# The attention's two query buffers in a pool of their own, over the index scores instead of over the layer input

## The chip, the cores and the metric

The kernel runs on one core of a Trainium2 chip. The metric is the device time of one execution in microseconds (us); the time of a kernel is the median of several runs on the same chip. The engines are named as in the profile: PE is TensorE, DVE is VectorE, ACT is ScalarE, POOL is GpSimd, SP is SyncE (here it only issues DMA transfers). Every engine takes its own instructions in the order in which the program holds them.

## The reference, cut to what matters

The model is a trunk of two layers over 1024 tokens of width 1024. Layer 0 projects the input once and feeds two mixers side by side: A, a delta-rule recurrence (RWKV-7, 8 heads of 64), and B, a sparse attention (8 query heads of 64 over one shared key and value, the 256 best keys of each query chosen by index scores). Layer 1 is a gated linear attention. The change concerns part B:

```python
def dsa_mix(q, ckv, qi, ki, wi, pos, kvn_g, wuk, wuv):
    c = rms_norm(ckv, kvn_g)
    k, v = partial_rope(c @ wuk, pos), c @ wuv
    q = partial_rope(q.reshape(Bn, T, B_HEADS, B_HEAD_DIM), pos)
    for each block of 128 queries:
        score = einsum('bqh,bqhs->bqs', wib, relu(einsum('bqhd,bsd->bqhs', qib, ki)))
        score = where(adm, score, -inf)                 # keys of this chunk of 64 and of those before
        vals, idx = top_k(score, 256)                   # the 256 best keys of each query
        s = einsum('bqhd,bqkd->bqhk', qb, k[idx]) * 64 ** -0.5
        out = einsum('bqhk,bqkd->bqhd', softmax(s), v[idx])
```

## The kernel before, in words

All is written in one function, `trunk`, with tiles from pools; a scheduler orders the instructions of each engine at build time by a model of its own, except where the code pins PE's order (`inorder`). Memory on the chip is handed out as on two stacks, one from each side. A pool that opens when another has closed takes over its place, and the first writer of a new tile waits until the last reader of the old tiles under it is done.

Layer 0 goes through these stages:

1. The input is transposed and split into a high and a low part, `xh` and `xl` (32 KB of each partition each, pool `big`). The index scores of query blocks 2 to 7 go into one tile `sc` (16.5 KB, pool `scp`). The queries of the attention are written to DRAM, `d_q`.
2. On PE, columns of the input projection follow one another: a block of weights is loaded (`wcols`, tile `craw`), split, and multiplied with `xh` and `xl` (`mm_cols`, lines 183 to 185, into the PSUM tile `dn`). Meanwhile DVE and ACT search the threshold of the 256 best scores in `sc` and write the masks `bias_s` (lines 670 to 747).
3. The last group of projections (`j = 3`, lines 750 to 765) gives the last head pair of part A. `operands` and `bonus` write its pieces to DRAM with DMAs that SP issues (`d_ar`, `d_bk`, `d_bd`, `d_bv`, `d_vt`; lines 534 to 613). Two gates come last (`gate`, lines 497 to 503: PE into `dn`, a tanh on ACT at line 501, a product on DVE at line 502 into the one buffer `sg`, then a DMA to `d_gate`).
4. The pools of these stages close, and the stage of the attention and the recurrence opens. On the right side lie `dsa` (keys, values, masks), then `scp`, then `big`, then the projection's weights. `dsa` stays. The attention's pool `at` opens in the place of the other three. It holds a small mask, the two query buffers `qT` (4 KB each), the score rows `p0` and `p1` and more. The recurrence's pool `rw` opens on the left side, over the tiles of stage 3; its first tiles (`GM`, `zi`, `XI`, `gn`, the first `RUV`) lie where `sg` lay.
5. PE starts with block 0 of the attention, in pinned order: `logits(0, h)` for 8 heads, two matmuls each (lines 835 and 836, query times `KH2` and `KL`), each head into one of three PSUM banks of the tag `s`. DVE reads each bank (line 837) and takes the row maximum, ACT the exponential (line 845). Then follow transposes of the weights (line 864), the logits of the next blocks, and from line 1016 the products of the recurrence. Block `i` needs `qT` of block `i`; `load_q(i)` takes the next of the two buffers and issues the load. The loads of blocks 0 and 1 are issued before the attention starts, that of block 2 once block 0's logits are done.
6. At the end of this stage the output projection's weights arrive (`wraw`, line 164; ACT's cast to `whi`, line 168), and its operands `yt` are loaded (line 1240), cast on ACT (line 1241) and subtracted on DVE (line 1242), between the last steps of the recurrence (lines 1087 to 1171).

SP takes its DMAs strictly in order, and a DMA that must wait for a buffer holds up all that stand behind it.

Of the kernel before, what the change touches and what calls it, by code (L numbers as in the profile page):

```python
# [9 lines left out]
F32R = mybir.dt.float32r  # L10
# [11 lines left out]
P = 128  # L22
# [35 lines left out]
ATS = (6, 7)  # L58
OG = (0, 0, 0, 0, 0, 0, 4, 4, 4, 0, 0)
ORD = (2, 3, 4, 9, 10, 5, 7, 11, 6, 8)  # L60
PG = [[], [0, 1], [], [], [2, 3], [4], [5], [6, 7]]
RK1 = 0

C_R, C_K, C_V, C_WA = 0, 512, 1024, 1536
# [9 lines left out]
def trunk(ctx: ExitStack, tc: tile.TileContext, x, positions, e_w_in, a_mu, a_w0, a_w2, a_a0, a_a2,  # L74
# [54 lines left out]
    def open_psum(name, dn, **bank):  # L129
        if psum:  # L130
            psum["ctx"].close()
        es = ExitStack()
        ctx.callback(es.close)
        psum.update(ctx=es, pool=es.enter_context(tc.tile_pool(name=name, bufs=1, space=PSUM)), dn=dn, bank=bank)
# [4 lines left out]
    def ptile(tag, bufs=None):  # L139
        return psum["pool"].tile([P, 512], F32, name=tag, tag=tag, bufs=psum["bank"].get(tag, 1))  # L140
# [93 lines left out]
    def scope():  # L234
        es = ExitStack()
        ctx.callback(es.close)
        return es
# [254 lines left out]
    def proj(c0):  # L492
        pt = dtile()
        mm_cols(pt, wcols(wr, ewi, c0), xh, xl)
        return pt

    def gate(z):
        g, j = divmod(z, 4)
        pt = proj((C_GB if g else C_GA) + j * P)
        o = gt.tile([P, SEQ], F32, name="sg")  # L500
        A.activation(o, pt, AF.Tanh, scale=0.5)
        V.scalar_tensor_tensor(o, o, 1.0, pt, op0=ALU.add, op1=ALU.mult)
        nc.sync.dma_start(d_gate[z], o)
# [6 lines left out]
    def shift_out(dst, pt, f):  # L510
        A.activation(dst, pt, AF.Copy, scale=drv[:, OMU + f:OMU + f + 1])
        V.scalar_tensor_tensor(dst[:, 1:SEQ], pt[:, 0:SEQ - 1], par[:, MU + f:MU + f + 1], dst[:, 1:SEQ],  # L512
                               op0=ALU.mult, op1=ALU.add)
# [15 lines left out]
    def st(name, w=SEQ, bufs=1, tag=None, pool=None):  # L529
        return (pool or t2).tile([P, w], F32, name=name, tag=tag or name, bufs=bufs)  # L530
# [9 lines left out]
    def norms(j, k):  # L540

        rn = st("rn")
        for h in range(2):
            sl = slice(h * 512, h * 512 + 512)
            sq = st("sq", 512)
            A.activation(sq, k[:, sl], AF.Square, scale=par[:, KKS + j:KKS + j + 1])
            pt = ptile("ix")
            PE.matmul(pt, bones, sq, start=True, stop=True)
            V.tensor_scalar(rn[:, sl], pt, 1e-24, None, op0=ALU.max)
        A.activation(rn, rn, AF.Ln)  # L550
        A.activation(rn, rn, AF.Exp, scale=-0.5)
        return rn

    def decays(j, h, pool):

        sl = slice(h * 512, h * 512 + 512)
        thw, tha = st("thw", 512, pool=pool), st("tha", 512, pool=pool)
        for th, row, bc in ((thw, 0, HW0), (tha, CH, HA0)):
            pt = ptile("ix")
            PE.matmul(pt, w2a2[row:row + CH, j * P:(j + 1) * P], wa[row:row + CH, sl], start=True, stop=True)  # L560
            A.activation(th, pt, AF.Tanh, scale=0.5, bias=drv[:, bc + j:bc + j + 1])
        ld = st("ld", 520, pool=pool).rearrange("p (c t) -> p c t", t=65)
        V.memset(ld[:, :, 0:1], 0.0)
        O(j, 10).tensor_scalar(ld[:, :, 1:65], c8(thw), DEC, DEC, op0=ALU.mult, op1=ALU.add)
        V.tensor_tensor_scan(flat(ld), flat(m0), flat(ld), 0.0, op0=ALU.mult, op1=ALU.add)
        Ei = c8(thw)
        A.activation(Ei, ld[:, :, 1:65], AF.Exp, scale=-1.0)
        A.activation(ld, ld, AF.Exp)
        A.copy(PC[:, j, h * 8:h * 8 + 8], ld[:, :, 64])
        return Ei, ld, tha  # L570
# [28 lines left out]
    def bonus(j, h, v, kk, brk):  # L599
        us = slice(h * 4, h * 4 + 4)  # L600
        pt = ptile("ix")
        PE.matmul(pt, brk, kk, start=True, stop=True)
        bv = kk
        V.tensor_mul(bv, pt, v[:, h * 512:h * 512 + 512])
        nc.sync.dma_start(d_bv[us, :, j, :].rearrange("u p t -> p u t"), bv.rearrange("p (u t) -> p u t", t=P))

    def tokens(j, h, v):
        pt = ptile("tr")
        for t in range(4):
            PE.transpose(pt[:, t * P:(t + 1) * P], v[:, (h * 4 + t) * P:(h * 4 + t + 1) * P], ident)  # L610
        vt = st("vt", 512, tag="sq")
        A.copy(vt, pt)
        nc.sync.dma_start(d_vt[h * 512:(h + 1) * 512, j * P:(j + 1) * P].rearrange("(t p) f -> p t f", p=P),
                          vt.rearrange("p (t f) -> p t f", f=P))

    def rates(j):
        brk = st("brk", P)
        V.tensor_scalar(brk, bones, par[:, RK + j:RK + j + 1], 0.5, op0=ALU.mult, op1=ALU.mult)
        return brk

    def shifted(f, c0, j):
        o = st("sh", bufs=3)
        shift_out(o, proj(c0 + j * P), f + j)
        return o
# [4 lines left out]
    for j in range(3):  # L629
        for z in PG[2 * j]:  # L630
            gate(z)
# [3 lines left out]
        for h in range(2):  # L635
            kk = operands(j, h, r, k, rn, decays(j, h, t2), t2)
            bonus(j, h, v, kk, brk)
            tokens(j, h, v)
        for z in PG[2 * j + 1]:
            gate(z)  # L640
# [94 lines left out]
    for i in SELO:  # L735
        n = P * (i + 1)
        xs = sc[:, rng(i)]
        z = slice(i - 2, i - 1)
# [13 lines left out]
    j = 3  # L752
    for z in PG[6]:
        gate(z)
    k = shifted(4, C_K, j)
    v = shifted(8, C_V, j)
    brk = rates(j)
    rn = norms(j, k)
    dec = [decays(j, 0, t2), decays(j, 1, t3)]
    r = shifted(0, C_R, j)  # L760
    for h in range(2):
        tokens(j, h, v)
    kks = [operands(j, h, r, k, rn, dec[h], (t2, t3)[h]) for h in range(2)]
    for h in range(2):
        bonus(j, h, v, kks[h], brk)
    for z in PG[7]:
        gate(z)
# [37 lines left out]
    inorder = (tc.keep_in_program_order if PIN_ else (lambda ins: ins))  # L805
    open_psum("ps1", 0, s=SB)
    at_ctx = scope()
    at = at_ctx.enter_context(tc.tile_pool(name="at", bufs=1, side="right"))
    RS = [slice(0, CH), slice(CH, P)]

    def aw(shape, name, bufs=1, dt=F32):
        return at.tile(shape, dt, name=name, tag=name, bufs=bufs)
# [5 lines left out]
    QT_, PT = {}, {}  # L818

    def load_q(i):  # L820
        if i < NT:
            QT_[i] = aw([P, 8, P], "qT", 2, F32R)
            nc.sync.dma_start(f32(QT_[i]), d_q[i])

    def logits(i, h):
# [24 lines left out]
    def weights(i, kt, s):  # L850

        if kt == 0 and s == 0:
            load_q(i + 2)
            ps, _, _, rsum = PT.pop(i)
            V.tensor_scalar(rsum, rsum, 2.0, None, op0=ALU.mult)
            V.reciprocal(rsum, rsum)
            rb = aw([P, 8, CH], "rb")
            A.copy(rb, rsum[:, :, None].to_broadcast([P, 8, CH]))
            g = aw([P, 4, P], "g")
            nc.sync.dma_start(g, d_gate[4:8, :, i * P:(i + 1) * P].rearrange("j p t -> p j t"))  # L860
            OUT[i] = dict(ps=ps, rb=rb, g=g, po=ptile("po"))
        pt = ptile(STB)
        for j in range(4):
            inorder(PE.transpose(pt[:, j * P:(j + 1) * P], OUT[i]["ps"][2 * j + s][:, kt * P:(kt + 1) * P], ident))  # L864
        pT = aw([P, 512], "pT", 4)
        (V.tensor_copy if (s + 2 * kt) % 4 in EVD else A.copy)(pT, pt)  # L866
        OUT[i][s] = pT
        if s and kt < i:
            ready.append((i, kt, (OUT[i][0], pT)))
# [382 lines left out]
    traced = nc.cur_bb.bb.instructions  # L1252
    first = len(traced)
    load_q(0)
    load_unit(0)
    load_at(0, 1)
    load_q(1)
    for h in range(8):
        logits(0, h)
# [335 lines left out]
```

## Time and profile before

| what | value |
|---|---|
| time of three runs, median (lowest to highest) | 1281.28 us (1278.65 to 1282.22) |
| the profiled execution: its time, its span | 1279.36 us, 1277.6 us |
| PE, DVE, ACT, POOL busy in that span | 92%, 60%, 47%, 34% |
| mean granted clock of PE | 0.962 |
| last matmul of the projection starts | 441.00 us |
| first matmul of the attention starts | 448.30 us |

Times in the rows of the timeline are microseconds from the start of the span, then the duration; in square brackets stands how long the engine stood idle just before and what ended that. In the rows of the windows stand the stretch, its length, the busy time of PE, PE's weight loads (PEld), DVE, ACT and POOL with the number of their instructions, PE's granted clock (1.00 is full speed), the busy share of the DMA engines and the GB/s that they moved. `SPq` is SP's queue: its rows are the issues of transfers, not the transfers.

### The profile page before, as it was taken

The page shows a single profiled execution, that of the slowest core. Times are in us where ns is not written, and L with a number is a line of the kernel's source. Part 1 is how long each engine was busy: PE and PEld are TensorE (multiplying, and loading weights), DVE is VectorE, ACT ScalarE, POOL GpSimd, SP SyncE. Part 2 cuts the span into 40 slices and gives each one's busy share as a digit, 9 for nine tenths or more (in the row PEclk, how much of TensorE's full clock was granted, in tenths as well). Part 3 has the DMA queues.
Part 4 walks back from the last instruction along what each step waited for, and adds up shares of the span by engine and source line. Part 5 has one row for each costly group of instructions (what it writes and reads, how often), then busy time and mean ns, then how long its engine had stood idle before and what let it go on. Part 6 is the DMA issues. An engine that isn't in the chain of part 4 may idle for free.

```text
span 1277.6 us, 22011 instructions
## 1 busy us (share of the span) xinstructions
PE 1178.4 (92%) x8125; PEld 939.3 (74%) x8125; DVE 771.6 (60%) x1832; ACT 599.8 (47%) x1256; POOL 436.4 (34%) x749
## 2 busy tenths in 40 slices
PE   7998799999998788989987699999999999998997
PEld 6986587767765566767775588777778888887785
DVE  5245868999998575677765545681701134534666
ACT  5347869798325265666764521223921043423100
POOL 3223823535464335354444700323033031232000
PEclk9999899999998978999999599999999999999999
DMA  6102321535352685443442847652022020014221
GB/s 214 42 1 83 100 58 34 167 81 164 84 156 58 168 227 134 105 121 87 112 121 52 248 144 242 192 181 73 1 66 57 9 67 1 17 50 140 83 99 50
DMA packets 164815, 130.61 MB, mean 102 GB/s; under 512 B 61428, under 2 KB 138276, under 8 KB 164708
## 3 DMA queue, kind: packets, MB, share of 16 engines
q1 hardware_dynamic: 161872, 122.72, 33.4%
q10 hardware_dynamic: 2836, 6.49, 1.6%
q8 instruction: 64, 1.05, 0.3%
q14 instruction: 43, 0.35, 0.1%
HBM read 86.18 MB, written 42.99 MB: 101 GB/s over the span
## 4 chain that ended last, share of the span: by engine, by line
PE 53%; DVE 18%; ACT 11%; issue 7%; DMA 7%; POOL 3%; SPq 1%; DVEq 0%; ACTq 0%; POOLq 0%
PE op L785 7%; PE s L785 7%; PE dn L183 3%; PE dn L184 3%; PE dn L185 3%; DVE fe L670 3%; PE gt L205 2%; PE gt L207 2%; PE gt L206 2%; ACT fs L700 2%; PE s L864 2%; PE po L887 2%; DVE sc L420 2%; DMA wraw<-in_e_w_in_dram 1%; ACT p L845 1%
## 5 line engine op out<-in xcount | busy, mean ns | idle before, releaser
L92 POOL TENSOR_TENSOR wlo<-wraw,whi 128x256 fp32r<-128x256 f32 (+1 forms) x160 | 117.7, 766 | 254.7 <-ACT whi L168 213.2
L183 PE MATMUL dn<-xh,chi 128*128 128x512 f32 x336 | 135.8, 404 | 2.4 <-DVE sh L512 1.8
L184 PE MATMUL dn<-xl,chi 128*128 128x512 f32 x336 | 134.8, 401 | 0.0
L185 PE MATMUL dn<-xh,clo 128*128 128x512 f32 x336 | 134.2, 399 | 0.0
L168 ACT CAST whi<-wraw 128x512 fp32r<-128x512 f32 (+1 forms) x80 | 48.6, 612 | 139.9 <-PE dn L184 63.4
L670 DVE TENSOR_SCALAR_CACHE_REDUCE fe<-sc,F 128x384 bf16<-128x384 f32 (+1 forms) x124 | 100.4, 810 | 3.1
L183 PEld LDWEIGHTS dn<-xh,chi 128*128 128x128 f32 x336 | 64.0, 191 | 22.1 <-issue 6.0
L185 PEld LDWEIGHTS dn<-xh,clo 128*128 128x128 f32 x336 | 64.1, 191 | 18.4 <-issue 5.3
L184 PEld LDWEIGHTS dn<-xl,chi 128*128 128x128 f32 x336 | 64.0, 191 | 17.5 <-issue 4.7
L92 POOL TENSOR_TENSOR clo<-craw,chi 128x256 fp32r<-128x256 f32 x84 | 75.5, 929 | 1.0
L420 DVE SCALAR_TENSOR_TENSOR sc<-rl,wi_s,sc 128x384 f32<-128x384 f32 (+5 forms) x42 | 45.2, 1077 | 23.5 <-ACT rl L415 21.1
L845 ACT ACTIVATE p<-p,am 128x128 f32<-128x128 f32 (+7 forms) x64 | 49.6, 776 | 19.6 <-DVE am L843 19.1
L837 DVE CUSTOM_DVE_ANT_0 p<-s,bias_s 128x512 f32<-128x512 f32 (+1 forms) x80 | 45.2, 593 | 22.0 <-PE s L836 21.6
L92 POOL TENSOR_TENSOR vg<-vg,sg 128x256 f32<-128x256 f32 x32 | 24.1, 774 | 99.5 <-DVE vg L1517 54.1
L193 POOL CAST chi<-craw 128x1024 fp32r<-128x1024 f32 x21 | 23.5, 1121 | 95.5 <-PE dn L184 60.8
L864 PE MATMUL s<-ident,p 128*128 128x128 f32 x288 | 48.4, 293 | 3.9 <-ACT pT L866 2.9
L205 PE MATMUL gt<-whi,hh 128*128 128x512 f32 x128 | 51.9, 406 | 0.0
L785 PE MATMUL op<-whi,yh 128*128 128x512 f32 x128 | 51.5, 404 | 0.0
L785 PE MATMUL s<-whi,yh 128*128 128x512 f32 x128 | 51.4, 402 | 0.0
L207 PE MATMUL gt<-whi,hl 128*128 128x512 f32 x128 | 51.2, 400 | 0.0
L206 PE MATMUL gt<-wlo,hh 128*128 128x512 f32 x128 | 51.0, 399 | 0.0
L785 PE MATMUL s<-wlo,yh 128*128 128x512 f32 x128 | 50.8, 397 | 0.0
(451 smaller groups left out, 3334.2 us busy)
## 6 DMA issues: line engine op xcount, KB each, us to landing
wraw<-in_o_w_in_dram SPq DMA_DIRECT2D x48, 256.0 KB
craw<-in_e_w_in_dram SPq DMA_DIRECT2D x21, 512.0 KB
xt<-in_x_dram SPq DMA_DIRECT2D x8, 512.0 KB
d_q<-qiT SPq DMA_DIRECT2D x8, 512.0 KB
d_gate<-sg SPq DMA_DIRECT2D x8, 512.0 KB
d_ar<-ar SPq DMA_DIRECT2D x8, 512.0 KB
qT<-d_q SPq DMA_DIRECT2D x8, 512.0 KB
AT<-d_ar SPq DMA_DIRECT2D x32, 128.0 KB
```

The costliest lines, as they stand in the source:

```text
L92: return [f(out[:, a:min(n, a + w)], *(z[:, a:min(n, a + w)] for z in ins)) for a in range(0, n, w)]
L183: PE.matmul(pst, wh[:, cs], ah[:, k, sl], start=(k == 0), stop=False)
L184: PE.matmul(pst, wh[:, cs], al[:, k, sl], start=False, stop=False)
L185: PE.matmul(pst, wl[:, cs], ah[:, k, sl], start=False, stop=(k == NK - 1))
L205: PE.matmul(pst, ah[:, k, sl], wh, start=(k == 0), stop=False)
L206: PE.matmul(pst, ah[:, k, sl], wl, start=False, stop=False)
L207: PE.matmul(pst, al[:, k, sl], wh, start=False, stop=(k == NK - 1))
L420: E.scalar_tensor_tensor(acc[:, a:b], r, w, acc[:, a:b], op0=ALU.mult, op1=ALU.add)
L670: V.tensor_scalar(junk[:, :P * (i + 1)], x, Ff[:, z] if b < 31 else 0.0, None, op0=ALU.is_ge, op1=ALU.add, accum_out=cnt[:, z])
L785: ins = PE.matmul(pt, a[:, k, :], b, start=(k == 0 and z == 0), stop=(k == NK - 1 and z == 2))
L845: A.activation(ps[k][:, :n], ps[k][:, :n], AF.Exp, scale=0.125, bias=m[:, k:k + 1], accum_out=rsum[:, k:k + 1])
L864: inorder(PE.transpose(pt[:, j * P:(j + 1) * P], OUT[i]["ps"][2 * j + s][:, kt * P:(kt + 1) * P], ident))
```

## The change

The two buffers `qT` leave the pool `at` and get a pool `qp`, opened just ahead of `at` on the same side. `qp` (8 KB) is thus the first to lie on `dsa`, in the place of `sc`; `at` follows above it. The total is the same. The two added loops over `PG[8]` and `PG[9]` run over empty lists and add no instruction.

```diff
-PG = [[], [0, 1], [], [], [2, 3], [4], [5], [6, 7]]
+PG = [[], [0, 1], [], [], [2, 3], [4], [5], [6, 7], [], []]
@@ the last head pair
     rn = norms(j, k)
+    for z in PG[8]:
+        gate(z)
     dec = [decays(j, 0, t2), decays(j, 1, t3)]
+    for z in PG[9]:
+        gate(z)
     r = shifted(0, C_R, j)
@@ the attention's pools
     at_ctx = scope()
+
+    qp = at_ctx.enter_context(tc.tile_pool(name="qp", bufs=1, side="right"))
     at = at_ctx.enter_context(tc.tile_pool(name="at", bufs=1, side="right"))
@@
     def load_q(i):
         if i < NT:
-            QT_[i] = aw([P, 8, P], "qT", 2, F32R)
+            QT_[i] = qp.tile([P, 8, P], F32R, name="qT", tag="qT", bufs=2)
             nc.sync.dma_start(f32(QT_[i]), d_q[i])
```

No instruction is added or taken away on any engine, and PE's order stays as it was. The order changes on the four other engines. The lines of the changed kernel are numbered six higher from the attention on (823 becomes 829).

On SP, behind the load of the last gate's weights (`craw`), before:

```order
L190 DMA craw<-in_e_w_in_dram 128x8x128
L613 DMA d_vt<-vt 128x4x128
L582 DMA d_ar<-ar 128x1024
L613 DMA d_vt<-vt 128x4x128
L582 DMA d_ar<-ar 128x1024
```

and changed:

```order
L190 DMA craw<-in_e_w_in_dram 128x8x128
L829 DMA qT<-d_q 128x1024 x2
L613 DMA d_vt<-vt 128x4x128
L582 DMA d_ar<-ar 128x1024
L613 DMA d_vt<-vt 128x4x128
```

The first two query loads now stand ahead of all transfers of the last head pair.

On SP, at the end of those transfers, before (`gn` in the profile is the small tile behind `gnp`, written on DVE at line 954):

```order
L534 DMA d_bd<-bk 64x1024
L536 DMA d_bd<-bk 64x8x64 x2
L605 DMA d_bv<-kk 128x4x128
L823 DMA qT<-d_q 128x1024 x2
L503 DMA d_gate<-sg 128x1024
L823 DMA qT<-d_q 128x1024
```

and changed:

```order
L534 DMA d_bd<-bk 64x1024
L536 DMA d_bd<-bk 64x8x64 x2
L605 DMA d_bv<-kk 128x4x128
L503 DMA d_gate<-sg 128x1024
L829 DMA qT<-d_q 128x1024
```

The write of the last gate now stands directly behind the last transfer of the head pair, and the load for block 2 behind it as before.

On ACT, in the last steps of the recurrence while the output projection's weights come in, before:

```order
L168 CAST whi<-wraw 128x512 x3
L1087 COPY Gs<-x 128x128
L168 CAST whi<-wraw 128x512
L1241 CAST yh<-yt 128x512
L1208 ACTIVATE yf<-x,gnp 128x128 x4
L1241 CAST yh<-yt 128x512
L1147 COPY RUV<-cb 64x4x64
L168 CAST whi<-wraw 128x512
L1097 COPY TT<-x 16x8x16 x2
L168 CAST whi<-wraw 128x512
L1241 CAST yh<-yt 128x512
L168 CAST whi<-wraw 128x512 x2
```

and changed:

```order
L168 CAST whi<-wraw 128x512 x2
L1093 COPY Gs<-x 128x128
L168 CAST whi<-wraw 128x512 x2
L1214 ACTIVATE yf<-x,gnp 128x128 x4
L1247 CAST yh<-yt 128x512 x2
L1153 COPY RUV<-cb 64x4x64
L1103 COPY TT<-x 16x8x16 x2
L168 CAST whi<-wraw 128x512 x3
L1247 CAST yh<-yt 128x512
L1177 COPY Y<-cb 64x256
L1177 COPY Y<-ca 64x256
L168 CAST whi<-wraw 128x512
```

The copy `Gs` moves ahead of the third cast, and the two copies `Y` (line 1171, now 1177), which before followed the last row shown with the fourth cast of `yt` between them, now stand together ahead of it. On SP the loads of the third and the fourth `yt` move back, behind some weights and the writes `d_y`.

## The prediction

> **What bounds the kernel now.** I read the chain of waits first, around the place where the change acts: the step from the projection (stage 3) to the attention.
>
> ```profile
> 442.23 0.47 SPq L823
> 442.75 5.25 DMA qT<-d_q
> 448.30 0.44 PE s L835
> ...
> 453.11 0.62 SPq L958
> ...
> 461.69 4.86 DMA g<-d_gate
> 466.57 0.69 DVE g L877
> ```
>
> The columns are start, length, what. The chain that ends last runs through the query load, the first logits, SP's queue and the load of the gate. So what the query load gives up here should move everything behind it, unless a link that does not depend on it takes over. PE's timeline shows the size:
>
> ```profile
> 441.00 0.39 PE L185 MATMUL dn<-xh,clo 128*128 128x512 f32 x1
> 448.30 0.44 PE L835 MATMUL s<-KH,qT 128*128 128x128 f32 x1 [6.91 <-DMA qT<-d_q]
> 448.76 0.41 PE L835 MATMUL s<-KH,qT 128*128 128x128 f32 x1
> ...
> 451.53 0.41 PE L836 MATMUL s<-KL,qT 128*128 128x128 f32 x1
> ...
> 461.04 1.13 PE L1016 MATMUL g<-AT,BK 128*128 128x128 f32 x8 [0.53 <-DMA BK<-d_bk]
> ```
>
> PE's last projection matmul ends at 441.39 and it then stands for 6.91 us until `qT` has landed. Third, SP's queue:
>
> ```profile
> 394.36 0.69 SPq L190 DMA_DIRECT2D craw<-in_e_w_in_dram  x1
> 418.81 0.37 SPq L613 DMA_DIRECT2D d_vt<-vt  x1
> ...
> 441.55 0.58 SPq L605 DMA_DIRECT2D d_bv<-kk  x1
> 442.23 1.31 SPq L823 DMA_DIRECT2D qT<-d_q  x2
> 443.73 0.35 SPq L503 DMA_DIRECT2D d_gate<-sg  x1
> 451.98 0.32 SPq L823 DMA_DIRECT2D qT<-d_q  x1
> ...
> 456.42 0.61 SPq L988 DMA_DIRECT2D BK<-d_bk  x1
> ```
>
> In the kernel before `qT` lies in the place of `xh`, which PE reads until its last projection matmul. So the two loads cannot start before 441.4, and SP issues them at 442.23, when its last transfer of the head pair is out.
>
> **The change, part by part.** *The loads move.* Now `qT` lies over `sc`, and `sc` has its last reader here:
>
> ```profile
> 399.86 0.08 DVE L742 DVE_READ_ACCUMULATOR fe<-sc,cand 128x1 f32 x1
> 441.43 1.02 ACT L501 ACTIVATE sg<-dn 128x1024 f32<-128x1024 f32 x1 [13.09 <-PE dn L185]
> 442.48 1.22 DVE L502 SCALAR_TENSOR_TENSOR sg<-sg,dn 128x1024 f32<-128x1024 f32 x1 [0.65 <-ACT sg L501]
> 449.00 0.29 DVE L837 CUSTOM_DVE_ANT_0 p<-s,cmask 128x128 f32<-128x128 f32 x1 [5.29 <-PE s L836]
> 450.60 0.20 POOL L930 MEMSET GM<- 128x128 f32 x1 [11.16 <-DVE mx L837]
> 452.72 0.21 DVE L954 TENSOR_SCALAR gn<-par 128x8 f32<-128x8 f32 x1 [0.25 <-issue]
> ```
>
> By the changed order the two loads stand behind `craw`, so SP reaches them at 395.1 and holds them until 399.94. Its next transfer, `d_vt`, is not due before 418.81: 18.9 us of cover, in which the DMA engines have little else to do. That costs nothing. Were the cover gone, `d_vt` and all behind it would wait (second rival). Both loads take the 5.25 us of the chain and are there some 36 us before PE asks.
>
> *What is late next on PE.* Head 0 of the logits can follow the last projection matmul at once. Heads go round three PSUM banks. The last gate's `dn` lies under one of them, and it is read until DVE's line 502 ends, at 443.70 (442.48 + 1.22). DVE also takes its line 837 only behind that, in order. So from the second head on the start is 443.75 where it was 448.76: 5.0 us. On DVE the first line 837 moves from 449.00 to 443.70: 5.3 us. Line 502 is bound by PE's last matmul, through ACT (441.43 + 1.02), and does not move.
>
> *What is late next on DVE and SP.* Behind the maxima DVE has `gn`, which lies on `sg`, the source of the last gate's write. POOL's `GM` lies there too and waited for the same write. (The profile names DVE as its releaser, but none of the maxima touches `GM`.) The windows show the DMA engines:
>
> ```profile
> 400.00:420.00 20.00, 20.00 (x58) 11.70 (x59) 13.87 (x17) 11.39 (x14) 6.08 (x5) 0.78 0.02 5
> 442.95:446.36 3.41, 0.00 (x0) 0.00 (x0) 0.75 (x1) 0.00 (x0) 0.00 (x0) 1.00 0.96 218
> 446.36:449.77 3.41, 1.47 (x7) 1.50 (x8) 0.65 (x5) 0.00 (x0) 0.00 (x0) 0.50 0.85 324
> 450.00:451.00 1.00, 1.00 (x7) 1.00 (x7) 0.88 (x9) 1.00 (x6) 0.40 (x3) 0.50 0.00 0
> ```
>
> They are busy from before 442.95 until about 450 and idle after, and `GM` starts at 450.60: the write had landed. Of what they moved, the two query loads are 1.05 MB (2 x 512 KB), which at 218 to 324 GB/s is 4.8 to 3.2 us. Without them the write lands 3.2 to 4.8 us earlier, and `GM` could start between 445.8 and 447.4. The other bound is the write alone, from its issue at 443.73: no row has it undisturbed; with the 4.86 us of the chain's `g` it lands at 448.6. DVE itself comes to `gn` 3.72 us after its first line 837 (449.00 to 452.72), now at 447.4: a move of 5.3, and of 4.1 if the write lands at 448.6. From `gn` on SP issues the small `gnp` loads, the recurrence's loads and `g` without a pause (453.11 to 461.69), so the whole piece up to `g` at 466.57 moves with it. I take 5.2 for the start, between PE's 5.0 and DVE's 5.3. Below it lies 4.1; above it DVE's own pace: eight times 0.29 for the maxima instead of 3.72 gives 6.7.
>
> *PE's clock.* It fell to half in the gap and came back only at 460:
>
> ```profile
> 395.17:398.58 3.41, 1.03 (x5) 0.53 (x3) 3.31 (x5) 3.41 (x7) 0.00 (x0) 1.00 0.86 203
> 399.00:400.00 1.00, 0.11 (x1) 0.11 (x1) 1.00 (x3) 0.84 (x2) 0.47 (x1) 0.50 0.00 0
> 456.60:460.02 3.42, 3.32 (x16) 3.03 (x15) 2.66 (x17) 3.24 (x14) 2.97 (x11) 0.50 0.72 218
> ```
>
> The granted clock was 1.00 up to 446.36 and 0.50 from there to 460.02. The new gap is only 2.3 us (441.39 to 443.70). The window from 395.17 to 398.58 ends in a gap of about that length, with PE busy for 1.03 of 3.41 us, and right after it the clock was 0.50. So I expect it to fall again, and count nothing for it. [...]
>
> *The order at the end of the recurrence.* Here ACT's and SP's rows change.
>
> ```profile
> 707.34 0.62 ACT L168 CAST whi<-wraw 128x512 fp32r<-128x512 f32 x1 [1.27 <-DMA wraw<-in_e_w_out_dram]
> 707.98 0.27 ACT L1087 COPY Gs<-x 128x128 f32<-128x128 f32 x1
> 719.61 0.62 ACT L1241 CAST yh<-yt 128x512 fp32r<-128x512 f32 x1 [1.13 <-DMA yt<-d_y]
> 720.25 0.37 ACT L1171 COPY Y<-ca 64x256 f32<-64x256 f32 x1
> ...
> 708.30 1.12 PE L1204 MATMUL x<-ident,Y 128*128 128x128 f32 x4 [4.13 <-ACT Gs L1087]
> 720.67 0.37 PE L1127 MATMUL ca<-RUV,AT 128*64 128x64 f32 x1 [3.19 <-ACT Y L1171]
> ...
> 714.23 0.38 SPq L1240 DMA_DIRECT2D yt<-d_y  x1
> ```
>
> `Gs` no longer stands behind a cast that waits for its DMA, which gives PE up to 1.9 us (1.27 + 0.62). The second `Y` no longer stands behind the fourth `yt`. But that `yt` took 5.4 us from issue to cast (714.23 to 719.61), its issue moves back by about 3 us, and its cast now stands ahead of the recurrence's next copy. So the most that is left is the 1.13 + 0.62 us of its wait and cast, less what comes back there. I take 0.3, between 1.2 and a loss of 0.5.
>
> The sum: 5.2 + 0.3 = 5.5 us. Against the profiled execution (1279.36 with what lies around its span of 1277.6) that is 1273.9; it ran 1.9 below the median of the runs. Against the median, 1281.28, it is **1275.8 us**. Between start and end I see nothing that is not itself behind the attention's start: weights, operands and the second layer all follow it.
>
> **The rivals.** *First, more.* The clock stays full over the new gap. Then the maxima run at DVE's pace, and the start is worth 6.7; with 1.2 from the end of the recurrence 7.9 us, 1273.4. For it: the gap is shorter than the 4.97 us (441.39 to 446.36) after which it fell before. Against: the row at 398.58.
>
> *Second, slower.* The loads are held not until 399.94 but until the projection's end. They would stand at the head of SP's queue with the 19 transfers from `d_vt` to the last `d_bv` behind them. These take 0.37 to 0.58 us each, up to 11 us from 441.4, and `bk` is written out twice from one buffer, two landings of about 4.8 one after the other. The loads for line 1016 would start near 462 instead of 456 and the end come 5.6 us later: 1286.9. It decides as soon as the release comes after 418.81. Against it: `qp` lies first in the place of `sc` and, with 8 of 16.5 KB, wholly within it.
>
> *Third, nothing to measure,* in two ways. The last gate's write may still land near 450.5, because its own way is that long; then `gn` moves by only 2.2 (452.72 to 450.5), 1279.1. Or the clock falls as before and comes back no sooner than at 460.02, while the work is 5.2 us ahead; then 5.2 us that ran at full clock run at half. Half of that hidden behind DVE and SP leaves 2.6, 1278.7. For the first: `GM` started 6.87 us after the write's issue. Against: 1.05 MB stood ahead of it.
>
> **How the numbers follow.** My forecast has a chance of 0.62, with a range of its own from 1273.8 to 1277.7 (gains of 7.5 to 3.6 us: 6.7 + 0.8 to 4.1 - 0.5). More has 0.12, nothing to measure 0.21 (0.13 and 0.08), slower 0.05. A change of this kernel by less than 0.3%, 3.8 us, can hardly be told from none, so faster means below 1277.4. Nearly all of the forecast (0.58) and the first rival make 0.70; the rest of the forecast, the third rival and a mild case of the second make 0.25; slower is 0.05. The range reaches down past the first rival, to 1272.0, and up over the third, to 1280.0.
>
> **What would show it.** SP issues both query loads near 400. PE stands for 2 to 3 us after line 185, released by DVE's line 502 and no longer by `qT`. The first line 837 starts near 443.7, `GM` and `gn` near 447.4, `g` is used near 461.4. At the end of the recurrence PE's waits of 4.13 and 3.19 us shrink together by less than 2 net. A wait of `d_vt` behind `qT`, `GM` still at 450, or a half clock past 460 would each make the prediction wrong, as would a new wait between 466 and 700.

## The result, and the profile after

| kernel | median of its runs | ratio to the kernel before, 95% interval |
|---|---|---|
| before | 1280.72 us (7 runs) | |
| changed | 1273.99 us (7 runs) | 0.9949 (0.9934 to 0.9965) |

The change takes 6.7 us off, 0.5%. Two more timings of the changed kernel gave 0.9948 (0.9927 to 0.9969) and 0.9935 (0.9914 to 0.9957): 5.6 and 6.4 us of the medians of the kernel before beside them (1281.54 and 1279.61). The prediction was 5.5 us.

First the chain of waits of the changed kernel at the place of the change (start, length, what):

```profile
443.31 1.03 ACT sg L501
444.36 1.23 DVE sg L502
...
459.14 4.78 DMA g<-d_gate
463.94 0.69 DVE g L883
```

The query load is gone from it. In its place stand the last gate's tanh and product. PE's timeline:

```profile
442.88 0.39 PE L185 MATMUL dn<-xh,clo 128*128 128x512 f32 x1
445.64 0.47 PE L841 MATMUL s<-KH,qT 128*128 128x128 f32 x1 [2.37 <-DVE sg L502]
...
446.13 0.42 PE L841 MATMUL s<-KH,qT 128*128 128x128 f32 x1
...
458.27 1.47 PE L1022 MATMUL g<-AT,BK 128*128 128x128 f32 x8
```

PE stands 2.37 us where it stood 6.91, and what ends the wait is line 502. This execution reached the end of the projection 1.88 us later than the one shown of before (442.88 against 441.00), in stages that the change does not touch. So every place behind it is read below from the start of the last projection matmul. SP's queue:

```profile
395.37 0.66 SPq L190 DMA_DIRECT2D craw<-in_e_w_in_dram  x1
401.02 0.81 SPq L829 DMA_DIRECT2D qT<-d_q  x2
419.49 0.37 SPq L613 DMA_DIRECT2D d_vt<-vt  x1
...
445.61 0.34 SPq L503 DMA_DIRECT2D d_gate<-sg  x1
```

Both query loads go out at 401.02, and 18.5 us pass until the next transfer is due. On DVE and POOL the first maximum, `gn` and `GM`:

```profile
446.37 0.29 DVE L843 CUSTOM_DVE_ANT_0 p<-s,cmask 128x128 f32<-128x128 f32 x1 [0.78 <-PE s L842]
448.41 0.20 POOL L936 MEMSET GM<- 128x128 f32 x1 [7.15 <-DVE mx L843]
449.76 0.17 DVE L960 TENSOR_SCALAR gn<-par 128x8 f32<-128x8 f32 x1
```

The table sets the profiles of this case side by side. Each column but one is the time from one PE matmul to another of the same number in PE's order, which is the same in all kernels but for a few neighbours that change places between 710 and 718 us: *gap* from the start of the last projection matmul to the start of the first logits; *start* from the same point to the first product (line 1016, now 1022); *g used* from the same point to the first use of `g` on DVE (line 877, now 883); *triangle* from there to the first triangular product (line 1085, now 1091, near 496); *570* a stretch of 100 matmuls that ends near 573; *end* 330 matmuls at the end of the recurrence, from 697 to 732 in the first profile of the changed kernel.

| kernel | gap | start | g used | triangle | 570 | end |
|---|---|---|---|---|---|---|
| before, two profiles | 7.30, 7.65 | 20.04, 20.38 | 25.57, 26.05 | 37.1, 37.3 | 13.0, 8.8 | 35.9, 35.8 |
| changed, three profiles | 2.76 in each | 15.39, 14.76, 13.90 | 21.06, 20.70, 21.42 | 37.7, 39.3, 39.1 | 8.5, 12.3, 10.1 | 35.2, 35.9, 36.0 |
| late issue | 7.22 | 19.91 | 25.80 | 38.6 | 8.6 | 35.7 |
| `dn` elsewhere | 2.76 | 14.23 | 19.65 | 37.9 | 10.8 | 35.8 |
| last gate in halves of one tile | 3.09 | 15.60 | 21.29 | 37.6 | 9.3 | 35.2 |
| last gate in two tiles, two profiles | 1.80 in each | 13.72, 13.87 | 19.10, 19.35 | 37.8, 38.1 | 10.2, 10.4 | 35.7, 35.4 |
| logits in the old pool | 0.23 | 14.21 | 19.95 | 41.6 | 9.2 | 36.0 |
| the same, `BD` held | 0.23 | 13.77 | 19.53 | 40.7 | 10.7 | 36.1 |
| two tiles and old pool, two profiles | 0.23 in each | 13.47, 13.83 | 19.31, 19.61 | 38.1, 38.3 | 8.9, 9.2 | 32.4, 32.4 |

The start gives 5.5 us (the mean of before, 20.21, less that of the three of the changed kernel, 14.68). Not all of it lasts: the first use of `g` comes 4.75 us sooner (25.81 less 21.06), and the first triangular product 4.0 us (start and triangle together are 57.1 and 57.7 before, 53.1, 54.1 and 53.0 after). The column 570 swings by 4 us in both kernels.

### The profile page after: what moved, and what is told of

Read it like the earlier page. It is cut to its first block, busy times and chain, and to the rows that moved or that the text cites. A ratio compares the mean times of both kernels' runs of the same rounds, so it can differ in the third digit from the quotient of the medians.

```text
span 1269.6 us, 22018 instructions
## 1 busy us (share of the span) xinstructions
PE 1173.5 (92%) x8125; PEld 936.0 (74%) x8125; DVE 772.7 (61%) x1832; ACT 599.8 (47%) x1256; POOL 438.5 (35%) x749
## 4 chain that ended last, share of the span: by engine, by line
PE 48%; DVE 16%; ACT 12%; issue 10%; DMA 7%; POOL 6%; SPq 1%; DVEq 0%; POOLq 0%; ACTq 0%
PE op L789 7%; PE s L789 7%; ACT fs L700 3%; DVE fe L670 3%; PE dn L185 3%; PE dn L184 3%; PE dn L183 3%; PE gt L206 2%; PE gt L205 2%; PE gt L207 2%; PE s L870 2%; DMA wraw<-in_e_w_in_dram 2%; POOL wlo L92 2%; PE po L893 1%; POOL qs L92 1%
## 5 line engine op out<-in xcount | busy, mean ns | idle before, releaser
L193 POOL CAST chi<-craw 128x1024 fp32r<-128x1024 f32 x21 | 22.8, 1085 | 93.3 <-PE dn L184 59.4
```

## The experiments

**The theory** was that the gain comes from the early issue of the two loads, after which the last gate's product on line 502 sets the start. The rivals were the other orders on DVE, ACT and SP, and the clock.

**The changed kernel again, and the kernel before again.** Nothing was edited. What was expected:

> The changed kernel once more, nothing edited. Theory (early loads): time near 1274 us, 0.995 of the kernel before; PE stands 2.3 to 2.5 us behind the last projection matmul, released by DVE's line 502. The two profiles at hand differ by about 5 us more in one place that the change does not touch, 568 to 580 us, where the kernel before ran at a granted clock near 0.57 and the changed one at 1.00. If that is chance, this profile may show a low clock there or not, and the stretches outside it repeat within 0.5 us. If it belongs to the change, the clock is 1.00 there again and the first matmul of the attention is again about 4.6 us earlier behind the projection than in the kernel before.

> The kernel before once more, nothing edited. PE stands 6.8 to 7.0 us behind the projection, released by qT. Whether the granted clock is near 0.57 from 572 to 580 us is chance by the theory, as the changed kernel has shown both.

The times of the first are in the section above. Its gap came out as expected; but outside 568 to 580 us the stretches did not repeat within 0.5 us (*start* 15.39 and 14.76, *triangle* 37.7 and 39.3). In the second PE stood 7.26 us, released by `qT`.

Of these two profiles, and of the first two, the windows with PE's granted clock (1.00 is full speed; the columns as in the table of the windows ahead of the prediction). First the changed kernel, first and second profile:

```profile
445.34:458.98 13.64, 12.21 (x49) 10.60 (x50) 10.18 (x68) 9.13 (x35) 9.33 (x34) 0.50 0.64 195
572.00:580.00 8.00, 8.00 (x100) 7.03 (x99) 6.96 (x33) 5.96 (x12) 0.74 (x3) 1.00 0.39 75
```

```profile
448.75:458.98 10.23, 9.35 (x39) 7.79 (x37) 8.20 (x57) 8.30 (x33) 7.66 (x29) 0.50 0.62 186
572.00:580.00 8.00, 8.00 (x65) 6.52 (x66) 4.02 (x17) 4.21 (x10) 4.09 (x12) 0.60 0.24 53
```

The kernel before, first and second profile:

```profile
572.00:580.00 8.00, 7.75 (x75) 6.23 (x71) 3.63 (x14) 4.15 (x9) 3.80 (x11) 0.57 0.31 68
```

```profile
572.00:580.00 8.00, 7.54 (x94) 6.16 (x95) 5.86 (x22) 6.79 (x15) 5.63 (x17) 1.00 0.29 69
```

From 572 to 580 each kernel has it both ways. The first two profiles alone would have put 4.5 us there (13.0 less 8.5) on the change's account; nothing shows it to be a part of it. Behind the projection the clock fell in each profile of the changed kernel, but at different times. The third profile was taken with the last timings:

> The changed kernel once more, nothing edited, for the comparison. 0.995 of the kernel before; PE stands 2.3 to 2.5 us behind the projection; the clock behind it may fall or stay, as the two profiles so far show both.

```profile
443.40:446.60 3.20, 2.80 (x18) 2.38 (x18) 2.52 (x25) 1.82 (x9) 0.04 (x1) 1.00 0.55 208
446.60:453.40 6.80, 6.05 (x23) 5.05 (x24) 5.57 (x35) 5.15 (x20) 6.03 (x23) 0.50 0.62 168
```

So the half clock lasted 13.6, 10.2 and 6.8 us in three executions of one program, and *start* took 15.39, 14.76 and 13.90 us: 0.6 to 0.9 us for each 3.4 us at half clock. That does not carry on: *g used* is 21.06, 20.70 and 21.42, in no such order. The gap was 2.37 us, released by line 502, each time.

**Late issue.** The buffers keep their new place, but the two loads stand behind the last `d_bv` again. No other engine's order moves.

```diff
-        nc.sync.dma_start(d_bv[us, :, j, :].rearrange(...), bv.rearrange(...))
+        BVW.append(nc.sync.dma_start(d_bv[us, :, j, :].rearrange(...), bv.rearrange(...)))
...
-            nc.sync.dma_start(f32(QT_[i]), d_q[i])
+            ins = nc.sync.dma_start(f32(QT_[i]), d_q[i]); after(BVW[-1] if i < 2 else None, ins)
```

> The query buffers keep their new place, but SP issues the first two query loads behind the last d_bv, where they stood before; PE, DVE, ACT and POOL keep the changed kernel's order. Theory (the early issue is what gains): PE again stands 6 to 7 us for qT, the start loses its 4.6 us, and only the other order at the end of the recurrence is left, 1.0 us: 1280.2 us, between 1279.0 and 1281.3. Rival (the new place and the other orders gain by themselves): 1274 to 1275 us.

Measured: 1278.49 us, 0.9981 (0.9965 to 0.9997). PE and SP:

```profile
439.67 0.39 PE L185 MATMUL dn<-xh,clo 128*128 128x512 f32 x1
446.89 0.44 PE L841 MATMUL s<-KH,qT 128*128 128x128 f32 x1 [6.83 <-DMA qT<-d_q]
```

```profile
440.87 1.44 SPq L829 DMA_DIRECT2D qT<-d_q  x2
442.41 0.40 SPq L503 DMA_DIRECT2D d_gate<-sg  x1
```

The wait for `qT` is back, and so is most of the time. Against the changed kernel of the same timing (0.9948) the late issue costs 0.0033 of 1281.5, 4.2 us; the spread of the single runs leaves some 3.4 us on either side of that. The sharper evidence is the stage: the two gaps differ by 4.46, *start* is 19.91 where the kernel before has 20.04 and 20.38, and *g used* 25.80. So the new place and the other orders by themselves do not shorten the start; the early issue that the place allows does. What is left against the kernel before, 2.4 us with an interval from 0.4 to 4.5, holds the 1.0 expected for the other orders; the time itself is 0.5 below the range that was expected. The column *end* shows 0.1 to 0.2 of it; where the rest would be, if it is real, no stage shows.

**`dn` elsewhere.** The PSUM tiles of the old pool are handed out in another order, so that the last gate's `dn` lies in banks 4 and 5. The prediction's step was that `dn` holds the second head because it lies under a bank of the logits.

```diff
-    open_psum("ps0", 2, tr=2, ix=2)
+    open_psum("ps0", 2, tr=2, ix=2); [ptile(z) for z in ("ix", "ix", "tr", "tr")]
```

> The changed kernel with the PSUM tiles of the stages before handed out in another order, so that the last gate's dn lies in banks 4 and 5, away from the three banks of the logits (0, 2, 1). Theory of the prediction (a shared bank holds the logits): PE's gap of 2.37 us goes to under 0.4 and head 0 to 2 run at once; DVE still comes to the maxima behind line 502, so the time is 0.4 to 0.8 us lower, 1273.3. Rival (the closing of the PSUM pool holds them: the first tile of the next pool waits for all readers of the pool before, wherever they lie): the gap stays at 2.3 to 2.5 us, released by line 502, 1274.0.

```profile
442.12 0.39 PE L185 MATMUL dn<-xh,clo 128*128 128x512 f32 x1
444.88 0.33 PE L841 MATMUL s<-KH,qT 128*128 128x128 f32 x1 [2.37 <-DVE sg L502]
```

1274.71 us, 0.9946 (0.9930 to 0.9962), and the same gap to the hundredth. The theory of the shared bank falls. What stands in this program is the rival: the first tile of a new PSUM pool waits for the last reader of the pool before it, wherever that lies.

**Logits in the old pool.** The counter-test: block 0's logits take tiles `ix` and `tr` of the old pool, and the new pool opens behind them. DVE still takes the maxima behind line 502.

```diff
-    open_psum("ps1", 0, s=SB)
...
-            pt = ptile("s")[:, :b - a]
+            pt = ptile("s" if i else ("ix", "tr")[h % 2])[:, :b - a]
...
-            V.tensor_tensor_reduce(ps[h][:, a:b], pt, ...)
+            after(GL[-1] if i == 0 else None, V.tensor_tensor_reduce(ps[h][:, a:b], pt, ...))
...
     for h in range(8):
         logits(0, h)
+    open_psum("ps1", 0, s=SB)
```

> The changed kernel with the logits of block 0 in PSUM tiles of the pool of the stages before (tags ix and tr), which closes only behind them; DVE still takes the maxima behind line 502. Theory (the closing of the pool holds the first logits): PE's gap behind the projection goes from 2.37 to under 0.2 us, four heads are ready when line 502 ends, the first maximum comes 0.8 us sooner and gn 1.0: 0.8 to 1.2 us less than the changed kernel, 1273.6 us. Rival (DVE's in-order queue alone holds the start, PE had time): gap gone, but gn, GM and g as before, 1274.5 us.

Measured: 1279.87 us, 0.9976 (0.9960 to 0.9992), which neither theory had (the kernel before took 1283.18 in this timing). PE, then DVE:

```profile
442.74 0.39 PE L185 MATMUL dn<-xh,clo 128*128 128x512 f32 x1
442.96 0.22 PE L841 MATMUL ix<-KH,qT 128*128 128x128 f32 x1
...
445.71 0.33 PE L841 MATMUL ix<-KH,qT 128*128 128x128 f32 x1 [1.74 <-DVE mx L843]
...
498.57 1.05 PE L1091 MATMUL x<-Tn,MAB 32*32 32x16 f32 x64 [7.60 <-DVE Tn L1086]
```

```profile
448.36 0.23 DVE L960 TENSOR_SCALAR gn<-par 128x8 f32<-128x8 f32 x1 [0.74 <-DMA d_gate<-sg]
```

The gap is gone, as the pool's closing demands: that step is shown. The first maximum comes 2.62 us behind the last projection matmul instead of 3.49. But the start does not gain by it. `gn` now waits for the last gate's write and comes 5.62 us behind the last projection matmul, against 6.88, 6.08 and 5.68 in the three profiles of the changed kernel. And 50 us later PE waits 7.60 us at line 1091, where the changed kernel waits 3.94 (3.67 to 4.54 in all profiles of this case but this one and the next). SP's order there had changed with the edit. The changed kernel's SP and POOL, then this kernel's:

```profile
476.13 1.10 SPq L1045 DMA_DIRECT2D Mt<-d_m  x2
477.28 0.59 SPq L995 DMA_DIRECT2D BD<-d_bd  x1
...
478.95 0.22 POOL L1058 TENSOR_TENSOR itmp<-Mt,Xt 128x15 f32<-128x15 f32 x1 [10.43 <-DMA Mt<-d_m]
```

```profile
474.87 0.54 SPq L995 DMA_DIRECT2D BD<-d_bd  x1
475.80 1.11 SPq L1045 DMA_DIRECT2D Mt<-d_m  x2
...
480.82 0.21 POOL L1058 TENSOR_TENSOR itmp<-Mt,Xt 128x15 f32<-128x15 f32 x1 [13.56 <-DMA Mt<-d_m]
```

With `BD` ahead of it `Mt` needs 5.0 us from issue to use (475.80 to 480.82) instead of 2.8. One more run holds `BD` behind `Mt`:

```diff
-        nc.sync.dma_start(BD.rearrange(...), d_bd[...])
+        after(MTI[-1] if u == 1 else None, nc.sync.dma_start(BD.rearrange(...), d_bd[...]))
...
-            nc.sync.dma_start(Mt[RS[z]].rearrange(...), dm.rearrange(...))
+            MTI.append(nc.sync.dma_start(Mt[RS[z]].rearrange(...), dm.rearrange(...)))
```

> The kernel with block 0's logits in the pool of the stages before (s_ps0_pin), with one thing held: SP issues the load BD of the second unit behind the two loads Mt again, as in the changed kernel (in s_ps0_pin BD stood ahead of them). Theory (that order cost the 4 us at the first triangular products): PE's wait there goes from 7.60 back to 3.7 to 4.3 us, and the time to 1274 to 1275. Rival (the logits in the old pool cost it by themselves): the wait stays above 7 and the time near 1279.9.

Measured: 1274.64 us, 0.9954 (0.9936 to 0.9973), beside 1279.61 for the kernel before. The time comes to where it was expected, though the intervals of the two ratios, 0.9976 and 0.9954, overlap. The wait goes only from 7.60 to 5.65:

```profile
499.94 1.05 PE L1091 MATMUL x<-Tn,MAB 32*32 32x16 f32 x64 [5.65 <-DVE Tn L1086]
```

So `BD` is at most a part of the cost. With it held, other loads further down SP's queue (`BK` near 491 us, `BD` near 505) went back to the changed kernel's order as well. The order still differs by one load of `AT` ahead of `d_m` and one of `RUV` ahead of `Mt`, which here needs 4.4 us from issue to use; whether these are the rest was not tried. What is shown is that an edit at the attention's start can lengthen a wait 50 us later by 3.7 us, with no other change there than rows that the scheduler placed otherwise.

**The last gate in halves.** If line 502 is the link, a shorter way from the projection's end to it should move the start. First in two halves of one tile (the edits of this part are abridged):

```diff
-        A.activation(o, pt, AF.Tanh, scale=0.5)
-        V.scalar_tensor_tensor(o, o, 1.0, pt, op0=ALU.add, op1=ALU.mult)
+        for s in (halves if z == 7 else whole): A.activation(o[:, s], pt[:, s], AF.Tanh, scale=0.5)
+        for s in (halves if z == 7 else whole): V.scalar_tensor_tensor(o[:, s], o[:, s], 1.0, pt[:, s], ...)
```

> The changed kernel with the last gate's tanh (line 501) and product (line 502) in two halves of 512 columns, so that the first halves run under the projection's second half. Theory (line 502 is the link that now sets the start): the last product ends about 1.0 us sooner behind the projection (half of 1.02 and half of 1.22, less some 0.1 of fixed cost), PE stands 1.3 to 1.5 us instead of 2.37, and all behind it moves by 1.0: 1273.0 us. Rival one (the way of the last gate's write, or SP, sets it): PE's gap shrinks, but GM and gn do not move, 1274.0. Rival two (clock): the shorter gap leaves the clock full past 445, and the start gains 2 us or more: 1272 or less.

1274.34 us, 0.9944 (0.9931 to 0.9957): nothing, and PE stands 2.70 us instead of the 1.3 to 1.5 expected. ACT shows why:

```profile
441.88 1.08 ACT L501 ACTIVATE sg<-dn 128x512 f32<-128x512 f32 x2 [12.53 <-PE dn L185]
```

Both halves of the tanh run behind the last matmul (which starts at 441.46), since the program lets the first wait for the whole tile `dn`. One half of the tanh and one of the product take 0.54 and 0.65 us here, 0.60 and 0.69 in the two tiles that follow: 0.06 and 0.16 us above half of the whole (1.03 and 1.23), where 0.1 was expected as fixed cost. Then in two PSUM tiles of their own:

```diff
+        pts = [ptile("tr"), ptile("tr")] if z == 7 else [proj(c0)]
+        [mm_fm(pt, wb, slice(0, P), xh, xl, q) for q, pt in enumerate(pts) if z == 7]
+        for q, pt in enumerate(pts): A.activation(o[:, q * n:q * n + n], pt, AF.Tanh, scale=0.5)
...
```

> The changed kernel with the last gate's two halves of 512 columns in two PSUM tiles of their own (tag tr), so that the first half's tanh and product can run while PE still multiplies the second. Theory (line 502 sets the start): behind the last projection matmul come one half of tanh (0.54 us) and one half of the product (0.65), PE stands 1.3 us instead of 2.37, and gn, GM and the first use of g follow 1.0 us sooner behind the projection: 1.0 us less than the changed kernel, 1273.5 us. Rival (the last gate's write or SP's queue sets it): the gap shrinks, but g is used no sooner, 1274.5 us.

> The last gate in two halves once more (gate_tr), beside the changed kernel on the same chip. Theory: PE again stands about 1.4 us behind the projection, and the time is 1.0 us below the changed kernel, with the clock's chance up to 2. If the halves are worth nothing: the same time as the changed kernel.

DVE and PE of the first of the two:

```profile
438.08 0.69 DVE L502 SCALAR_TENSOR_TENSOR sg<-sg,tr 128x512 f32<-128x512 f32 x1 [3.52 <-ACT sg L501]
441.30 0.69 DVE L502 SCALAR_TENSOR_TENSOR sg<-sg,tr 128x512 f32<-128x512 f32 x1 [0.22 <-ACT sg L501]
...
445.48 0.23 DVE L960 TENSOR_SCALAR gn<-par 128x8 f32<-128x8 f32 x1 [0.65 <-DMA d_gate<-sg]
```

```profile
440.25 0.39 PE L185 MATMUL tr<-xh,clo 128*128 128x512 f32 x1
442.05 0.33 PE L841 MATMUL s<-KH,qT 128*128 128x128 f32 x1 [1.41 <-DVE sg L502]
```

The gap shrinks by 0.96 us, as line 502 demands, and *start* to 13.72 and 13.87 us, 0.9 below the mean of the changed kernel. `g` is used 19.10 and 19.35 us behind, against 20.70 to 21.42; but `dn` elsewhere, with the changed kernel's order on every engine, had 19.65, so little of that is clear. `gn` now stands for the last gate's write, so behind line 502 this write is the next link. It is issued 0.96 us sooner and lands hardly sooner: `GM` and `gn` start 5.23 and 5.59 us behind the last projection matmul in these two profiles, where `GM` started at 5.53, 5.53 and 5.68 in the changed kernel's. The times, 0.9937 (0.9915 to 0.9960) and 0.9941 (0.9921 to 0.9962), can't be told from the changed kernel's.

**Two tiles and old pool together** (for the logits `ix` and the free `dn` instead of `ix` and `tr`):

> Both edits together: the last gate in two halves, and the logits of block 0 in the pool of the stages before (tags ix and dn). If both links count by themselves: gap under 0.2 us, first maximum 1.8 us sooner behind the projection than in the changed kernel, 1272.6 us. If only one of them can count, as both end in line 502: 1273.5 us. If the granted clock stays full because PE hardly stands: 2 us less still, 1271.

> Halves and old pool together once more (gate_tr_ps0), beside the changed kernel on the same chip. If the earlier ratio, 0.9925, was no chance: 2 to 3 us below the changed kernel. Theory (the last gate's write, on which gn and GM wait, is the next link): no more than gate_tr, 1.0 us below.

1271.41 us, 0.9925 (0.9901 to 0.9948), and 1271.76 us, 0.9929 (0.9906 to 0.9952). That is the best time of all, but its intervals overlap those of the changed kernel. *Start* gains nothing over the two tiles alone (13.47 and 13.83), as the write demands. PE no longer stands behind the projection, and no pause up to the fall of the clock is longer than 0.78 us; still the clock did not stay full, the case that the first expectation had named. PE's longest pause, and the windows around the fall, in the second profile:

```profile
443.79 0.33 PE L841 MATMUL ix<-KH,qT 128*128 128x128 f32 x1 [0.78 <-DVE mx L843]
```

```profile
446.00:447.00 1.00, 0.49 (x2) 0.14 (x1) 0.00 (x0) 1.00 (x7) 0.00 (x0) 1.00 0.89 307
448.00:449.00 1.00, 1.00 (x6) 0.88 (x4) 0.78 (x4) 0.47 (x1) 0.90 (x5) 0.50 0.44 122
```

The half clock lasted 6.8 us in both profiles. What differs is *end*, 32.4 instead of 35.2 to 36.0. ACT at the end of the recurrence, the changed kernel and then this one (its second profile):

```profile
709.26 0.62 ACT L1247 CAST yh<-yt 128x512 fp32r<-128x512 f32 x1 [0.41 <-DMA yt<-d_y]
709.90 0.37 ACT L1177 COPY Y<-cb 64x256 f32<-64x256 f32 x1
710.29 0.37 ACT L1177 COPY Y<-ca 64x256 f32<-64x256 f32 x1
```

```profile
705.64 0.36 ACT L1177 COPY Y<-cb 64x256 f32<-64x256 f32 x1
706.02 0.37 ACT L1177 COPY Y<-ca 64x256 f32<-64x256 f32 x1
...
706.97 0.62 ACT L1247 CAST yh<-yt 128x512 fp32r<-128x512 f32 x1
```

Here the two copies `Y` stand ahead of the cast that waits for its DMA. That the 3.3 us of *end* come from this one row, and not from the other casts and loads that moved with it, was not tried.

## Why the prediction was right, step by step

The prediction was 1275.8 us with a gain of 5.5; measured were 1273.99 and gains of 5.6 to 6.7. Places are given from the start of the last projection matmul (441.00 before, 442.88 after).

- **The loads.** Right. They were to be issued near 400 and went out at 401.02, with 18.5 us of cover (18.9 was said). The rival in which they block SP did not come.
- **Head 0 "can follow the last projection matmul at once".** Wrong. It starts 2.76 us behind, released by line 502. The shared bank was the wrong reason; the closing of the old pool holds every head. This step made the PE term 5.0; the first logits moved by 7.30 - 2.76 = 4.5, since the first head's 0.49 us (445.64 to 446.13) now stands behind line 502 too.
- **DVE.** The first line 837 was to move by 5.3, from 8.00 to 2.70 us. It came at 3.49 (446.37 - 442.88), as it waits for that same head: 4.5.
- **The write of the last gate.** `GM` was to start 4.8 to 6.4 us behind the last matmul (445.8 to 447.4) and did at 5.53 in this profile. The write needs 2.80 us from its issue (445.61) to `GM` (448.41) where it needed 6.87, so the query loads ahead of it had cost 4.1, within the 3.2 to 4.8 of the prediction. That `GM` waits for the write was inferred there against the name in the profile; the second profile of the changed kernel names it (`450.26 0.20 POOL L936 MEMSET GM<- 128x128 f32 x1 [7.17 <-DMA d_gate<-sg]`). `gn` was to come at 6.4 and came at 6.88; it moved by 4.8 instead of 5.3. In the kernels with the short gap the profile names this write itself as what ends the wait of `gn`.
- **The start.** 5.2 was taken for all up to the use of `g`. It moved from 25.57 (466.57 - 441.00) to 21.06 (463.94 - 442.88), 4.5, within the bounds of 4.1 and 6.7; the mean of all profiles is 4.75. Over all profiles *start* gives 5.5. What it has above the use of `g` goes with the shorter half clock in two of the three, and is not seen at the use of `g`.
- **The clock.** It was to fall again, and fell in all three profiles, so the first rival's full clock did not come. The half clock lasted 13.6, 10.2 and 6.8 us, against 13.7 in the first profile of before (446.36 to 460.02). In two of three it was thus shorter, which PE's first product shows and the use of `g` does not; so as far as the profiles show it was right to count nothing for it. In the row that the prediction leaned on, PE had stood 2.38 us when the clock fell at 398.58; the whole pause was 3.69 us, ended at 399.89. A short gap did not keep the clock full here: one of 2.37 us was followed by the fall each time, and so were pauses of 0.78 us at most in the kernel with two tiles and the old pool.
- **The end of the recurrence.** 0.3 was said, between -0.5 and 1.2. *End* took 35.9 and 35.8 before, and 35.2, 35.9 and 36.0 after: 0.2 on the mean. The two waits that were to shrink, 4.13 and 3.19 us, did so by 3.0 to 4.0 together; the next waits of PE, for `RUV` and `Zs`, grew from 1.50 and 0.52 to 2.1 and 1.2 to 1.7.
- **"Between start and end I see nothing".** Open. The column *triangle* is longer in all three profiles of the changed kernel (37.7 to 39.3) than in both of before (37.1 and 37.3), so that 0.4 to 2.2 us of the start are given back there; why was not tried. The late issue has 38.6, so the early issue is not needed for it. The column *570* moves by 4 us between executions of one kernel, in both directions.

The stages that were predicted give 4.0 us up to the first triangular product and 0.2 at the end, 4.2 in all; the medians give 5.6 to 6.7, and the interval of the first timing runs from 4.5 to 8.5 (0.35% and 0.66% of 1280.7). So the mechanism and the time are as predicted, but that the sum of 5.5 came so near to the timings is in part luck: its term for the start was 0.5 us too large at the use of `g` and 1.2 at the first triangular product, and 1.4 to 2.5 us of the measured gain lie in no stage that the profiles show to repeat. Whether the other orders hold a part of them stays open; the late issue's 0.9981 leaves room for it.

## What to carry to other kernels

When a wait is taken away, read the next one from the wait list of the instruction and not from the addresses: here the first tile of a new PSUM pool waited for the last reader of the whole pool before it, wherever its banks lay (2.37 us with `dn` in either place). Compare stages between two marks of the engine's own order, over several profiles, before a difference far from the edit is put on its account, and follow a gain to the next marks: of 5.5 us at PE's first product 4.0 were left at the first triangular one. And where a scheduler places SP's and ACT's rows, look after each edit at the rows that wait for a DMA: here a wait 50 us behind the edit was 3.7 us longer, with a load moved ahead of two others on its way, and in another kernel the end of the recurrence, where such a cast had moved, was 3.3 us shorter.

## What the runs showed of the hardware

One program got its half clock for 6.8, 10.2 or 13.6 us behind the same gap of 2.37 us. A long gap is not needed for it: with no pause above 0.78 us the clock fell as well, 5.8 and 5.4 us behind the last projection matmul in two profiles, and stayed at half for 6.8. Nor does the fall go with one busy time just before: of the 3.20 us ahead of the fall PE was busy for 0.00 in the first profile of before (fall at 446.36), for 1.13 in the first of the changed kernel (445.34) and for 2.80 in its third (446.60). What the clock counts is left open. At the half clock the heads of the first profile took 0.43 us each (446.13 to 446.56 and on), at the full clock those of the third 0.22 to 0.33. The stretch near 572 alone moves by 4 us with the clock between executions of an unchanged kernel (13.0 and 12.3 us in the two profiles with a clock of 0.57 and 0.60 from 572 to 580, before and changed, 8.8 and 8.5 in the two with 1.00); single runs of the changed kernel went from 1268.7 to 1278.1 us.

A write of 512 KB (`d_gate`) needed 6.87 us from its issue to the first use of its buffer with two loads of the same size ahead of it in the queue, and 2.80 us without them.
